# A decoder layer on one core: elementwise work moved from GpSimd to VectorE, gate products in two accumulators, LayerNorm's affine on ScalarE, conditioning dots respread

## The chip, the cores and the metric

The kernel runs on one core of a Trainium2 chip. A core has TensorE (PE in the profile, matrix products; PEld is its loading of weights), VectorE (DVE), ScalarE (ACT), GpSimd (POOL) and SyncE (SP), which here only issues transfers. Each has a queue of its own and works it off in order; they meet through semaphores. The metric is the device time of one execution in microseconds (us).

## The reference

One layer of a decoder for 1024 positions of width 1024, in float32. A mixer with a convolution and an attention branch, then a SwiGLU network; both sit between RMS norms whose shift, scale and gate come from a conditioning vector c.

```python
c_act = silu(c)
mod = c_act @ ada_w + ada_b                  # 6 x 1024 numbers
sh1, sc1, ga1, sh2, sc2, ga2 = split(mod, 6)
h = rmsnorm(x, pre_mix_g) * (1 + sc1) + sh1
proj = h @ w_in                              # conv inputs, q k v, two gates of 1024
u = u_val * sigmoid(u_gate)
u = silu(layernorm(causal_depthwise_conv(u, conv_w, conv_b)))   # width 512
y_conv = u @ w_conv_out
o = stick_breaking_attention(q, k, v)        # 8 heads of 64
y_att = o @ w_att_out
merged = sigmoid(g_conv) * y_conv + sigmoid(g_att) * y_att
x = x + ga1 * rmsnorm(merged @ w_o, post_mix_g)
h = rmsnorm(x, pre_ffn_g) * (1 + sc2) + sh2
gate, up = split(h @ w_ffn_in, 2)            # 2816 each
x = x + ga2 * rmsnorm((silu(gate) * up) @ w_ffn_out, post_ffn_g)
```

## The kernel before

**Splits.** A float32 product is made of three products of a rounded type: each operand is split into a high half (a rounding copy on ScalarE) and a low half (the difference, on another engine), and hi·hi, hi·lo and lo·hi are accumulated. Names that end in `hi` and `lo` are such halves. `load_w` (L161) loads a weight tile (128 x 1024, tile `raw`) and makes its halves; its low half is on GpSimd unless the caller names an engine. `w_op` (L297) does the same for a 128 x 512 operand that is in SBUF already, where the low half has the tile's own name (`a`, `s2o`).

**Stages.** Activations lie with channels on partitions and positions along the row; `CH` = 512 positions are half a row, `T` = 1024 a whole one. In order of time: a prologue (c, the first norm) to 60 us; the heads of the attention, with the convolution and other products as filling in TensorE's queue, to 446; the plain gates (`pg`) and the first two products of the other gates (`k1`, `k2`) to 512; the other five products of each gate pair, beside which the LayerNorm runs, to 598; `y_conv` (`pyc`) to 646; the attention's projection and the merge (`pya`) to 690; w_o (`pwo`) to 793; the first network product to 1237; and its second in three sweeps, `pa`, `pb` and `pc`, and an end, to 1476.

**Gates.** Six of the eight pairs of gate tiles are computed with seven products of half-sized operands instead of eight. `a11`, `a12`, `a21`, `a22` are the quarters of a weight tile, `s1` to `s4` sums of them, `T1` to `T4` (made from `f`) sums of quarters of h. `k1` and `k2` are done early and give `ee`; `other_five` (L586) does the rest, each product of 12 matmuls into a PSUM bank of its own out of four that rotate (`bkg`), and VectorE adds a bank to `v`, `w_` or `c21` as soon as it is done.

**LayerNorm.** `ln_all` (L626) sums channels on GpSimd (`la`), takes mean and variance by products with ones, normalizes on VectorE (`cr`), applies gain and bias on VectorE (L657), the sigmoid on ScalarE (`csig`) and the product (`csil`) on VectorE, one of four on GpSimd. `chi` and `clo` are its halves.

**Merge.** For each of eight tiles, VectorE multiplies the two halves of `pya` with the gate (`sga`), adds them to `yc` (the second half on GpSimd, L724), and the sum is split into `mhi` and `mlo` for w_o.

**Conditioning.** Each of 48 columns of `mod` is a dot of a 128 x 1024 tile of ada_w with c on VectorE (`dot_c`, L131; tiles `ada`). 0 to 15 are done in the prologue; 16 to 39 beside `y_conv` (two a step) and the merge (one a step); 40 to 47, the last gate's, in w_o.

**Order.** Loads are issued on SP's queue, stores on GpSimd's. The order of each engine's queue is set by a list scheduler of the language (`schedule_with_timeline_sim`), which simulates the program as written and takes priorities (`high_priority`); a change in one place moves rows elsewhere. Only the first network product is pinned in an order written by hand. Tiles come from pools with few buffers, and a load into a tile waits until the buffer's last reader is done: the tag `wraw` has three, `whi` and `wlo` three each. In the sweeps, `pull` issues the next steps' loads ahead, and `prep` makes the operands (`gt`, `gb`, `wa`); `w2f` are weight sums stored earlier.

Of the kernel before, what the change touches and what calls it, by code (L numbers as in the profile page):

```python
# [45 lines left out]
LN_DVE0 = ()  # L46
LN_DVE1 = ()
SILU_POOL = (3,)
# [10 lines left out]
FIN_AT = (8, 8)  # L59
W2_AT = tuple(range(EARLY, EARLY + FH))  # L60
# [13 lines left out]
def tile_block(ctx: ExitStack, tc: tile.TileContext, xT, vecs, crow, ada1, ada2, win, wv, wcv, wat, wo, w1, w2, cvw, out):  # L74
# [26 lines left out]
    def load(dst, src):  # L101
        nc.sync.dma_start(dst, src)
# [58 lines left out]
    def load_w(src, name, hi_eng=act, lo_eng=pool):  # L161
# [130 lines left out]
    HK = KT // 2  # L292
    GPAIRS = GORDER[:KT - NPL]
# [9 lines left out]
    def prod0(bank_, w, b):  # L303
        for j in range(HK):
# [7 lines left out]
            for s, (st, mv) in enumerate(((0, 0), (0, 1), (1, 0))):  # L312
                pe.matmul(bank_, w[st][:, cols], mvs[mv], start=(j == 0 and s == 0),
                          stop=(j == HK - 1 and s == 2))

    with ExitStack() as sC:
        pc = mkpool(sC, "pc")
        with ExitStack() as sA:
# [196 lines left out]
            for i in GPAIRS:  # L515
# [4 lines left out]
                prod0(k1, w_op(f"a11_{i}", raw[:, :CH], act, pool), "B11")  # L520
# [3 lines left out]
                prod0(k2, w_op(f"a12_{i}", raw[:, CH:], act, pool), "B21")  # L524
# [5 lines left out]
    with ExitStack() as sG:  # L530
# [55 lines left out]
        def other_five(i):  # L586
# [7 lines left out]
            s2o = w_op(f"s2o_{i}", s2, act, pool)  # L594
# [31 lines left out]
        def ln_all():  # L626
# [27 lines left out]
            for ct in range(CONVT):  # L654
                a = cacc[ct]
                g, b_ = vec[:, C_LNG + ct:C_LNG + ct + 1], vec[:, C_LNB + ct:C_LNB + ct + 1]
                dve.tensor_scalar(a, a, g, b_, op0=ALU.mult, op1=ALU.add)  # L657
                sg = hp.tile([P, T], F32, tag="act", name=f"csig{ct}")
                act.activation(sg, a, AF.Sigmoid, bias=0.0, scale=1.0)
# [6 lines left out]
        a2 = deque(range(2 * KT, 5 * KT))  # L666
# [9 lines left out]
        def y_conv(n):  # L676
            if n % 2 == 0:
                wcs[n // 2] = load_w(wcv[n // 2], f"wc{n}")
# [828 lines left out]
```

## Time and profile before

| | us |
|---|---|
| runs | 1476.1, 1477.73, 1478.54 (median 1477.73) |
| the profiled execution | 1477.53 |
| its span (first to last instruction) | 1475.6 |
| PE busy | 1396.4 (95%) |
| DVE busy | 1024.5 (69%) |
| ACT busy | 651.3 (44%) |
| POOL busy | 342.8 (23%) |
| mean granted clock of TensorE | 0.983 of full speed |

Busy times are sums of instructions of the profiled execution; the span is the time base of all stretches quoted below. Of POOL's time the heads' products (`be`, L459) take 100.6 us; they stay where they are.

### The profile page before, as it was taken

Reading aid. Unit: us, or ns where it says so; the run is one execution under the profiler, and the core shown is the slowest. Engines: PE = TensorE matmul, PEld = TensorE weight load, DVE = VectorE, ACT = ScalarE, POOL = GpSimd, SP = SyncE. Lnnn points to the kernel's source line nnn. Section 1 sums busy time; section 2 is a strip of 40 time slices with the busy share of each in tenths; the row PEclk is TensorE's granted clock in tenths of the full one; section 3 lists DMA queues with packets and bytes.
Section 4 is the critical chain, followed back from the end, with each engine's and each line's share of the span. In section 5 each row is a group of like instructions: output and inputs, shape, how many; then the busy total and the mean of one; then the engine's idle time right before and its main releaser. Section 6 shows DMA issues by size and latency. Waiting matters only on the chain.

```text
span 1475.6 us, 18944 instructions
## 1 busy us (share of the span) xinstructions
PE 1396.4 (95%) x6888; PEld 1164.5 (79%) x6888; DVE 1024.5 (69%) x1434; ACT 651.3 (44%) x1139; POOL 342.8 (23%) x353
## 2 busy tenths in 40 slices
PE   4999999999999899898999899999999997999996
PEld 3898788898888678686877578888888886888886
DVE  7775364545658689879668697777777765764457
ACT  5365465354554355312346543334444443433441
POOL 0042344323454564524010110001111110000000
PEclk8999999999999999999999999999999998999999
DMA  9203213122143744775823454446777759365833
GB/s 382 90 29 91 96 58 129 58 73 86 43 143 114 236 157 159 283 257 193 310 104 122 149 171 172 157 152 240 251 256 253 243 189 363 114 238 193 286 125 114
DMA packets 89356, 253.74 MB, mean 172 GB/s; under 512 B 9520, under 2 KB 19888, under 8 KB 88240
## 3 DMA queue, kind: packets, MB, share of 16 engines
q1 hardware_dynamic: 73648, 199.06, 39.8%
q0 software_dynamic: 15616, 53.49, 9.7%
q8 instruction: 54, 0.88, 0.2%
q14 instruction: 38, 0.31, 0.1%
HBM read 186.97 MB, written 65.54 MB: 171 GB/s over the span
## 4 chain that ended last, share of the span: by engine, by line
PE 30%; issue 14%; DVE 8%; POOL 3%; DMA 3%; ACT 2%; POOLq 0%; DVEq 0%; ACTq 0%
PE ka L1227 8%; PE ka L1108 6%; PE pb L1227 4%; PE kc L1108 4%; PE pwo L795 3%; PE pa L1227 2%; DMA ada<-in_ada_dram 2%; DVE ada L133 1%; POOL w_d L105 1%; PE ke L960 1%; POOL g_d L105 1%; DVE wo_lo L167 1%; DVE y L844 0%; PE psx L1004 0%; DVE yc L724 0%
## 5 line engine op out<-in xcount | busy, mean ns | idle before, releaser
L459 POOL TENSOR_TENSOR be<-be,ka 128x127 f32<-128x127 f32 (+2 forms) x96 | 100.6, 1062 | 163.0 <-DVE ka L457 90.0
L457 DVE TENSOR_TENSOR_SCAN ka<-ka 128x128 f32<-128x128 f32 (+2 forms) x96 | 106.6, 1134 | 45.5 <-ACT ka L453 45.4
L473 DVE TENSOR_TENSOR alo<-tr,ahi 128x512 fp32r<-128x512 f32 x80 | 53.1, 684 | 53.0 <-ACT ahi L472 52.3
L453 ACT ACTIVATE ka<-z 128x128 f32<-128x128 f32 (+2 forms) x96 | 47.5, 496 | 61.2 <-PE z L452 32.8
L105 POOL DMA_DIRECT2D g_d<-uw x22 | 12.0, 544 | 239.2 <-DVE uw L1180 239.2
L472 ACT ACTIVATE ahi<-tr 128x512 fp32r<-128x512 f32 x80 | 46.2, 602 | 47.0 <-PE tr L469 31.2
L1227 PE MATMUL ka<-gt,w2f 128*128 128x512 f32 x264 | 63.4, 389 | 0.0
L133 DVE SCALAR_TENSOR_TENSOR ada<-ada,cb 128x1024 f32<-128x1024 f32 x32 | 48.5, 1522 | 20.0 <-DMA ada<-in_ada_dram 19.9
L795 PE MATMUL pwo<-mhi,wo_hi 128*128 128x512 f32 x128 | 52.2, 409 | 6.7 <-ACT mhi L157 4.0
L1227 PEld LDWEIGHTS ka<-gt,w2f 128*128 128x128 f32 x264 | 49.5, 188 | 10.3
L960 PE MATMUL ke<-b,we_hi 128*128 128x512 f32 x144 | 48.0, 416 | 5.4 <-ACT we_hi L157 5.4
L795 PE MATMUL pwo<-mlo,wo_hi 128*128 128x512 f32 x128 | 51.1, 399 | 1.7 <-DVE mlo L623 1.7
L795 PE MATMUL pwo<-mhi,wo_lo 128*128 128x512 f32 x128 | 50.9, 398 | 0.5 <-DVE wo_lo L167 0.5
L469 PE MATMUL tr<-ident,be 128*128 128x128 f32 x288 | 48.8, 273 | 0.5 <-DVE alo L473 0.4
L454 ACT ACTIVATE be<-z 128x128 f32<-128x128 f32 (+2 forms) x96 | 46.9, 499 | 4.0 <-PE tr L469 3.8
L479 PE MATMUL av<-alo,vst 128*128 128x256 f32 x160 | 42.9, 294 | 2.2 <-DVE alo L473 2.1
L478 PE MATMUL av<-ahi,vst 128*128 128x256 f32 x160 | 44.8, 296 | 0.2 <-DVE oT L483 0.2
L359 PE MATMUL pcv<-ph,cvw 128*128 128x128 f32 x320 | 41.7, 276 | 1.6 <-DMA ph<-v_d 1.6
L1108 PE MATMUL kb<-b,a 128*128 128x512 f32 x156 | 41.5, 389 | 0.0
L359 PEld LDWEIGHTS pcv<-ph,cvw 128*128 128x128 f32 x320 | 39.1, 192 | 2.7 <-DMA ph<-v_d 1.7
L1227 PE MATMUL ka<-gb,wa 128*128 128x512 f32 x132 | 33.5, 402 | 7.9 <-ACT gb L157 7.9
L1213 DVE TENSOR_TENSOR gt<-X,gt 128x512 fp32r<-128x512 f32 x33 | 22.6, 691 | 26.0 <-ACT gt L157 25.9
(520 smaller groups left out, 4208.4 us busy)
## 6 DMA issues: line engine op xcount, KB each, us to landing
w_d<-w2o POOLq DMA_DIRECT2D x44, 512.0 KB, 7.1
w2f<-w_d SPq DMA_DIRECT2D x44, 512.0 KB, 4.4
ada<-in_ada_dram SPq DMA_DIRECT2D x32, 512.0 KB, 4.4
w1g<-in_w_dram SPq DMA_DIRECT2D x22, 512.0 KB, 3.6
w1u<-in_w_dram SPq DMA_DIRECT2D x22, 512.0 KB, 6.1
w2r<-in_w_dram SPq DMA_DIRECT2D x44, 256.0 KB, 3.8
cvw<-in_cvw_dram SPq DMA_DIRECT2D x20, 512.0 KB, 3.5
ada_w<-in_ada_dram SPq DMA_DIRECT2D x8, 1024.0 KB, 13.2
```

The costliest lines, as they stand in the source:

```text
L133: dve.scalar_tensor_tensor(w, w, 1.0, cb, op0=ALU.mult, op1=ALU.mult, accum_out=mod[:, col:col + 1])
L359: pe.matmul(cv[:, gi * TM:(gi + 1) * TM], wts[n][:, at:at + P], ph[:, g, SH - 1 - d:SH - 1 - d + TM], start=(d == 0), stop=(d == SH - 1))
L453: act.activation(kap[:, s_lo:s_hi], z[:, zo:zo + w], AF.Sigmoid, bias=0.0, scale=-0.125)
L454: act.activation(beta[:, :w], z[:, zo:zo + w], AF.Sigmoid, bias=0.0, scale=0.125)
L457: dve.tensor_tensor_scan(rev, rev, rev, init, op0=ALU.mult, op1=ALU.bypass)
L459: pool.tensor_tensor(beta[:, :m], beta[:, :m], kap[:, s_lo + 1:s_lo + 1 + m], op=ALU.mult)
L469: pe.transpose(tr[:, o:o + P], src, ident)
L473: dve.tensor_tensor(alo, tr, ahi, op=ALU.subtract)
L795: pe.matmul(bank_, st[:, cols], mv[k][:, cs], start=(k == 0 and q == 0), stop=(k == KT - 1 and q == 2))
L960: pe.matmul(kb, wf[st][:, cols], t[:, mv], start=(j == 0 and q == 0), stop=(j == HK - 1 and q == 2))
L1108: pe.matmul(bank_, st[:, cols], t[:, mv], start=(first and j == 0 and s == 0), stop=(j == HK - 1 and s == 2), skip_group_check=not first)
L1227: pe.matmul(dst, w[st][:, cols], g[mv], start=first and s == 0, stop=last and s == 2, skip_group_check=more)
```

## The change

Elementwise instructions that GpSimd had go to VectorE: the low halves of weights (13 in the heads' part, four each of the plain gates, the convolution's and the attention's projection), of the early gate operands (`a11`, `a12`, 12) and of the gate sums (`s1`, `s2`, `s3`, 18); the 12 sums of the LayerNorm; one silu product; two of `olo`; eight adds of the merge. GpSimd keeps the products of the heads, two low halves of `wv`, and all stores. The gate products accumulate in two banks a pair, `ka` (T2, then T3 and T4 on top) and `kc` (T1, then B22), VectorE reading a bank between. LayerNorm's gain and bias become ScalarE's: once inside the sigmoid, once as a pass of its own. Of the dots, 16 to 31 are done beside `y_conv`, none in the merge, 32 to 39 in w_o, 40 to 47 in sweep `pb` at its second to fifth step, with the conditioning vector loaded anew for each step.

```diff
-LN_DVE0 = ()
-LN_DVE1 = ()
-SILU_POOL = (3,)
+LN_DVE0 = (0, 1)
+LN_DVE1 = (0, 1)
+SILU_POOL = ()
+DOT_AT = "pb"
...
+    GP = dve
...
-    def load_w(src, name, hi_eng=act, lo_eng=pool):
+    def load_w(src, name, hi_eng=act, lo_eng=dve):
...
-    def prod0(bank_, w, b):
+    def prod0(bank_, w, b, first=True):
...
-                pe.matmul(bank_, w[st][:, cols], mvs[mv], start=(j == 0 and s == 0),
-                          stop=(j == HK - 1 and s == 2))
+                pe.matmul(bank_, w[st][:, cols], mvs[mv], start=(first and j == 0 and s == 0),
+                          stop=(j == HK - 1 and s == 2), skip_group_check=not first)
...
-                prod0(k1, w_op(f"a11_{i}", raw[:, :CH], act, pool), "B11")
+                prod0(k1, w_op(f"a11_{i}", raw[:, :CH], act, dve), "B11")
...
-            s2o = w_op(f"s2o_{i}", s2, act, pool)
+            s2o = w_op(f"s2o_{i}", s2, act, GP)
...
-            k6 = bkg(f"k6_{i}")
-            prod0(k6, s2o, "T2")
-            dve.tensor_tensor(v, k6, p1, op=ALU.add)
-            k7 = bkg(f"k7_{i}")
-            prod0(k7, w_op(f"s3o_{i}", s3, act, pool), "T3")
-            dve.tensor_tensor(w_, k7, v, op=ALU.add)
-            k4 = bkg(f"k4_{i}")
-            prod0(k4, w_op(f"a22_{i}", a22, act, dve), "T4")
-            dve.tensor_tensor(c21, k4, w_, op=ALU.add)
+            ka, kc = bkg(f"ka_{i}"), bkg(f"kc_{i}")
+            prod0(ka, s2o, "T2")
+            dve.tensor_tensor(v, ka, p1, op=ALU.add)
+            prod0(kc, w_op(f"s1o_{i}", s1, act, GP), "T1")
+            dve.tensor_tensor(w_, kc, p1, op=ALU.add)
+            prod0(ka, w_op(f"s3o_{i}", s3, act, GP), "T3", False)
+            dve.tensor_tensor(w_, ka, w_, op=ALU.add)
+            sig_out(w_, 2 * i + 1, 1)
+            prod0(kc, w_op(f"s4o_{i}", s4, act, dve), "B22", False)
+            dve.tensor_tensor(v, kc, v, op=ALU.add)
+            sig_out(v, 2 * i, 1)
+            prod0(ka, w_op(f"a22_{i}", a22, act, dve), "T4", False)
+            dve.tensor_tensor(c21, ka, p1, op=ALU.add)
             sig_out(c21, 2 * i + 1, 0)
-            k5 = bkg(f"k5_{i}")
-            prod0(k5, w_op(f"s1o_{i}", s1, act, pool), "T1")
-            dve.tensor_tensor(v, k5, v, op=ALU.add)
-            dve.tensor_tensor(w_, k5, w_, op=ALU.add)
-            k3 = bkg(f"k3_{i}")
-            prod0(k3, w_op(f"s4o_{i}", s4, act, dve), "B22")
-            dve.tensor_tensor(v, k3, v, op=ALU.add)
-            sig_out(v, 2 * i, 1)
-            sig_out(w_, 2 * i + 1, 1)
...
-                dve.tensor_scalar(a, a, g, b_, op0=ALU.mult, op1=ALU.add)
-                act.activation(sg, a, AF.Sigmoid, bias=0.0, scale=1.0)
+                act.activation(sg, a, AF.Sigmoid, bias=b_, scale=g)
+                act.activation(a, a, AF.Identity, bias=b_, scale=g)
...
-        a2 = deque(range(2 * KT, 5 * KT))
+        a2 = deque(range(2 * KT, 4 * KT))
...
-                (pool if c and n < Y_POOL else dve).tensor_tensor(y[:, cs], y[:, cs], sg[c], op=ALU.add)
+                dve.tensor_tensor(y[:, cs], y[:, cs], sg[c], op=ALU.add)
...
-            ada2_dots(last, 1)
...
-                for col in ((), (40, 41), (42, 43), (44, 45), (46,), (47,), ())[n]:
+                for col in ((), (32, 33), (34, 35), (36, 37), (38,), (39,), ())[n]:
...
+        def gate_dots(n):
+            cbt = wp.tile([P, D], F32, tag="wraw", name=f"cb_{n}")
+            load(cbt, cb_d)
+            for q in range(2):
+                w = wp.tile([P, D], F32, tag="wraw", name=f"ada2_{40 + n + q}")
+                load(w, ada2[24 + n + q])
+                dot_c(w, cbt, 40 + n + q)
...
+                if name == DOT_AT and 0 < j <= KT // 2:
+                    gate_dots(2 * j - 2)
```

The built programs show where the rows went. First VectorE's queue at the early gate products, where `ee_i` is the sum of pair i's first two products, `f` and `T` the sums of h, `a_i` the low half of an early gate operand; before:

```order
L565 TENSOR_TENSOR f_3_4727<-f_3_4728,f_3_4727 128x512
L525 TENSOR_TENSOR ee_1_4454<-k_1_4473,ee_1_4453 128x512
L566 TENSOR_TENSOR f_3_4728<-f_3_4728,f_3_4727 128x512
L567 TENSOR_TENSOR f_3_4728<-f_3_4728 128x512
L556 TENSOR_TENSOR T2o_4735<-f_3_4728,T2o_4735 128x512
L556 TENSOR_TENSOR T3o_4738<-f_3_4727,T3o_4738 128x512
L592 TENSOR_TENSOR gs_0_4759<-gw0b 128x512
```

And the same place of the changed kernel:

```order
L567 TENSOR_TENSOR f_3_4727<-f_3_4728,f_3_4727 128x512
L568 TENSOR_TENSOR f_3_4728<-f_3_4728,f_3_4727 128x512
L302 TENSOR_TENSOR a_4_4579<-ew_4574,a_4_4579 128x512
L569 TENSOR_TENSOR f_3_4728<-f_3_4728 128x512
L558 TENSOR_TENSOR T2o_4735<-f_3_4728,T2o_4735 128x512
L558 TENSOR_TENSOR T3o_4738<-f_3_4727,T3o_4738 128x512
L558 TENSOR_TENSOR T1o_4741<-f_3_4727,T1o_4741 128x512
L302 TENSOR_TENSOR a_4_4597<-ew_4574,a_4_4597 128x512
L527 TENSOR_TENSOR ee_1_4454<-k_1_4473,ee_1_4453 128x512
L558 TENSOR_TENSOR T4o_4744<-f_3_4728,T4o_4744 128x512
```

The low halves `a` stand between the sums, and the add of pair 1 has moved behind the sums of h that it stood before. (On TensorE, 126 matmuls of the plain gates stand behind the last product of the attention instead of 93.) Second, VectorE's queue in the merge; before:

```order
L723 TENSOR_TENSOR sga_1_5885<-pya_1_5887,sga_1_5885 128x512
L133 SCALAR_TENSOR_TENSOR ada_33_5922,mod<-ada_33_5922,cb 128x1024
L724 TENSOR_TENSOR yc_5543<-yc_5543,sga_0_5884 128x512
L723 TENSOR_TENSOR sga_0_5931<-pya_0_5933,sga_0_5931 128x512
L723 TENSOR_TENSOR sga_1_5932<-pya_1_5934,sga_1_5932 128x512
L133 SCALAR_TENSOR_TENSOR ada_34_5969,mod<-ada_34_5969,cb 128x1024
L623 TENSOR_TENSOR mlo_5919<-yc_5543,mhi_5918 128x1024
L724 TENSOR_TENSOR yc_5585<-yc_5585,sga_0_5931 128x512
```

After:

```order
L720 TENSOR_TENSOR sga_0_5939<-pya_0_5941,sga_0_5939 128x512
L720 TENSOR_TENSOR sga_1_5940<-pya_1_5942,sga_1_5940 128x512
L620 TENSOR_TENSOR mlo_5936<-yc_5561,mhi_5935 128x1024
L721 TENSOR_TENSOR yc_5597<-yc_5597,sga_0_5939 128x512
L721 TENSOR_TENSOR yc_5597<-yc_5597,sga_1_5940 128x512
L168 TENSOR_TENSOR wo_0_lo<-wo_0_raw,wo_0_hi 128x1024
```

Both adds of a step stand in VectorE's queue now, and the dots are gone from between them. Third, VectorE's queue where sweep `pa` ends and `pb` begins (`wa_10` are the low halves of `pa`'s last weight tile, `gt` those of `pb`'s operands), after:

```order
L134 SCALAR_TENSOR_TENSOR ada_40_10881,mod<-ada_40_10881,cb_10879 128x1024
L1208 TENSOR_TENSOR gt_0_10835<-X_10330,gt_0_10835 128x512
L1265 TENSOR_TENSOR X_10330<-Y_10341,X_10330 128x512
L1265 TENSOR_TENSOR X_10330<-X_10330 128x512
L1214 TENSOR_TENSOR wa_10_10742<-wa_10679,wa_10_10742 128x512
L1208 TENSOR_TENSOR gt_0_10839<-X_10330,gt_0_10839 128x512
L134 SCALAR_TENSOR_TENSOR ada_41_10884,mod<-ada_41_10884,cb_10879 128x1024
L1214 TENSOR_TENSOR wa_10_10748<-wa_10679,wa_10_10748 128x512
```

And on SP's queue there, where the loads of the dots stand between those of `w2f`:

```order
L103 DMA cb_10879<-cb_d 128x1024
L103 DMA w2f_0_10718<-w_d_122 128x1024
L103 DMA w2f_0_10720<-w_d_122 128x1024
L103 DMA ada_40_10881<-in_ada_dram 128x1024
L103 DMA w2f_1_10736<-w_d_123 128x1024
L103 DMA w2f_1_10738<-w_d_123 128x1024
L103 DMA ada_41_10884<-in_ada_dram 128x1024
L103 DMA cb_10924<-cb_d 128x1024
```

The second low half of `wa_10` stands behind two dots, the second of which waits for a load that can only start when the first dot has freed its buffer; before, no dot stood in this stretch.

More of the change, by code (lines that the diff above doesn't have):

```diff
@@ L523, in tile_block @@
                 k2 = bank(f"k2_{i}")
-                prod0(k2, w_op(f"a12_{i}", raw[:, CH:], act, pool), "B21")
+                prod0(k2, w_op(f"a12_{i}", raw[:, CH:], act, dve), "B21")
                 dve.tensor_tensor(e[1], k2, e[0], op=ALU.add)
@@ L677, in y_conv @@
             if n % 2 == 0:
-                wcs[n // 2] = load_w(wcv[n // 2], f"wc{n}")
+                wcs[n // 2] = load_w(wcv[n // 2], f"wc{n}", act, dve)
             y = flat(ot(f"yc{n}"))
@@ L863, in tile_block @@
                         dot_c(w, cb2, col)
-        add_bias(40, 48)
-        fold_gate(gpost2, 40, C_POST2)
+        add_bias(32, 40)
+        fold_scale(scale2, 32, C_PRE2)
         begin = len(nc.cur_bb.bb.instructions)
@@ L1388, in tile_block @@
             act.activation(c22[n], kc[n], AF.Copy)
+        add_bias(40, 48)
+        fold_gate(gpost2, 40, C_POST2)
         sweep("pc", prep3, (False, False), kc)
```

7 lines of the change are left out of this document (3 added, 4 removed).

## The prediction

> **What bounds the kernel now.** I read the engines' shares first, then the busy time by stage, then TensorE's waits, and last the rows of the engines waited for.
>
> ```profile
> PE 1396.4 (95%) x6888; PEld 1164.5 (79%) x6888; DVE 1024.5 (69%) x1434; ACT 651.3 (44%) x1139; POOL 342.8 (23%) x353
> 60.00:455.00 395.00, 388.39 (x2415) 339.76 (x2414) 222.51 (x274) 206.91 (x423) 152.88 (x124) 1.00 0.25 81
> 455.00:500.00 45.00, 40.07 (x169) 32.36 (x168) 40.89 (x40) 20.00 (x38) 23.45 (x23) 0.96 0.47 154
> 500.00:590.00 90.00, 89.65 (x388) 72.48 (x387) 73.77 (x90) 43.09 (x68) 49.39 (x47) 1.00 0.52 177
> 590.00:608.00 18.00, 11.67 (x38) 7.21 (x37) 17.05 (x15) 8.79 (x11) 10.03 (x8) 0.91 0.68 265
> 608.00:690.00 82.00, 81.59 (x360) 67.19 (x358) 67.75 (x83) 17.06 (x17) 32.50 (x14) 1.00 0.76 260
> 690.00:712.00 22.00, 15.70 (x52) 11.55 (x53) 18.57 (x23) 6.92 (x8) 6.56 (x3) 0.77 0.34 109
> 980.00:1237.00 257.00, 257.00 (x1136) 212.87 (x1135) 190.68 (x303) 114.55 (x205) 38.47 (x72) 1.00 0.69 240
> 1307.00:1370.00 63.00, 63.00 (x280) 52.16 (x279) 35.33 (x53) 22.97 (x39) 0.00 (x0) 1.00 0.72 246
> ```
>
> The first row is the page's; the others give a stretch, its length, the busy time (and instructions) of PE, PEld, DVE, ACT and POOL, the granted clock, the DMA share and GB/s. TensorE is the bound: it is full in most stages, and a change of the other engines can only win back its holes. Full pace is 257.00 / 1136 = 0.226 us for a matmul. By that count the early k products (455 to 500) lose 45 − 169 × 0.226 = 6.8 us, the passage from the gate products to the convolution's projection (590 to 608) 18 − 38 × 0.226 = 9.4, and the passage from the attention's projection to w_o (690 to 712) 22 − 52 × 0.226 = 10.2. In those three VectorE is busy for 91%, 95% and 84% of the time. The 395 us of heads lose only 395 − 388.39 = 6.6. So 26.4 us lie where this change works.
>
> ```profile
> PE k L313 <- DVE ee L525: 4.9, 2, 2.6
> PE pwo L795 <- ACT mhi L157: 4.0, 2, 3.8
> PE pyc L178 <- ACT chi L157: 2.9, 2, 2.7
> PE k L313 <- DVE s4o L300: 2.1, 1, 2.1
> PE pwo L795 <- DVE mlo L623: 1.7, 2, 1.2
> 495.70:499.10 3.40, 3.40 (x10) 2.71 (x9) 1.41 (x1) 1.25 (x3) 3.17 (x4) 0.51 1.01 342
> 598.10:601.50 3.40, 3.21 (x7) 2.05 (x8) 2.74 (x3) 3.20 (x4) 2.55 (x2) 0.51 0.49 191
> 697.00:707.30 10.30, 6.09 (x14) 4.43 (x15) 9.72 (x12) 3.06 (x3) 4.18 (x2) 0.51 0.03 12
> ```
>
> The waits (us, times, longest) name what TensorE stood for: results of VectorE, or a rounding on ScalarE that itself stood for VectorE. The three stretches of half clock say what the waits cost on top: 3.4 us at 0.51 loses 1.7 us, 10.3 us loses up to 5.
>
> The Trainium skill, "TensorE: Matmul & The Clock Gate", section "What's actually happening", lets the clock halve after at least one idle window of about 3.4 us. Here longest waits of 2.6 and 2.7 us already stand near a half-clock stretch, so the trace halves earlier than that page says. By its rule a residual wait under 3.4 us would cost itself alone, and the sum below would be 1.7 us lower.
>
> **The k products.** The two waits on `ee` (4.9 us) are adds that come late in VectorE's queue because their neighbours are stretched.
>
> ```profile
> 469.96 1.71 POOL L300 TENSOR_TENSOR a<-ew,a 128x512 fp32r<-128x512 f32 x1
> 470.43 1.78 DVE L564 TENSOR_TENSOR f<-f 128x512 f32<-128x512 f32 x1
> 474.09 0.69 DVE L566 TENSOR_TENSOR f<-f,f 128x512 f32<-128x512 f32 x1
> L525 DVE TENSOR_TENSOR ee<-k,ee 128x512 f32<-128x512 f32 x6 | 4.1, 686 | 2.9 <-DMA s_d<-ee 2.9
> L300 POOL TENSOR_TENSOR a<-ew,a 128x512 fp32r<-128x512 f32 x10 | 15.1, 1515 | 16.9 <-ACT a L157 9.0 <-issue 7.8
> L643 DVE TENSOR_TENSOR cr<-cr,lm 128x512 f32<-128x512 f32 x8 | 8.5, 1125 | 0.0
> L562 DVE TENSOR_TENSOR f<-hhi,hlo 128x1024 f32<-128x1024 f32 x3 | 5.8, 1949 | 0.0
> L657 DVE TENSOR_SCALAR cr<-cr,vec 128x1024 f32<-128x1024 f32 x4 | 4.1, 1050 | 0.0
> L662 DVE TENSOR_TENSOR csil<-cr,csig x3: 2144/2195/3630, 585.5 to 593.2; 128x1024 f32<-128x1024 f32 x3
> ```
>
> The first three rows are the timeline, the rest groups of 455 to 608 (behind the bar: us busy, mean ns) and, last, a tile's row (min, median and max ns). Beside a GpSimd elementwise an add of VectorE takes 1.78 us; alone 0.69. The add that reads PSUM (`ee`, 686 ns) is not touched. So a 128x512 op taken from GpSimd frees up to 1.1 us of VectorE and costs 0.69 there.
>
> For 455 to 608 as a whole, VectorE's busy time before is 40.89 + 73.77 + 17.05 = 131.7 us. Added: ten `a` lows, 18 gate-operand lows and 12 LayerNorm adds, 40 × 0.69 = 27.6; three convolution-weight lows at 1.22 (the `mlo` row below, 128x1024) 3.7; one silu product, 2.2 (the median of its three siblings). Removed: L657, 4.1; six gate adds, 4.1. The stretching goes: summed over the 21 groups of this view that exceed 0.69 or 1.22 us without reading PSUM (L643 is the first, at 8 × 0.44; L562 gives 3 × 0.73) it is about 30 us. That leaves 131.7 + 33.5 − 8.2 − 30 = 127 us. TensorE's own work there is (169 + 388 + 38) × 0.226 = 134.5 us, and about 33 matmuls of plain gates, which the new order leaves until after the last attention product, add 7.5 us of cover at its start. VectorE thus has less to do than TensorE, not more. I take the full 6.8 us back; the bounds are 0 (the `a` lows now stand ahead of `ee` in one queue) and 6.8.
>
> **LayerNorm and the two-bank gate products.** ScalarE gains four 128x1024 passes, about 1.06 us each (`mhi` below is such a pass), and has 18 − 8.79 = 9.2 us free in 590 to 608, so they fit; yet they stand in the chain sigmoid, product, rounding, low half, four times, in which VectorE has 4 × (2.2 + 1.22) = 13.7 us and ScalarE 4 × 3 × 1.06 = 12.7. Two banks instead of five make the third product of a pair wait until VectorE has read the first's bank; between them stands the other bank's product of 12 × 0.226 = 2.7 us, or another pair's, against a read of 0.69. That is covered while VectorE lags under 2 us. The end of the chain has no such cover to spare, so I leave one wait of 1.7 us and one 3.4 us stretch at half clock, 1.7 us: 3.4 of 9.4 remain, 6.0 come back. Bounds: all 9.4 back; or 5 lost, if each of the last pairs waits about one read.
>
> **Attention's projection.** The merge loop is where VectorE is the bound.
>
> ```profile
> 658.65 1.28 DVE L723 TENSOR_TENSOR sga<-pya,sga 128x512 f32<-128x512 f32 x2
> 701.86 0.68 DVE L723 TENSOR_TENSOR sga<-pya,sga 128x512 f32<-128x512 f32 x1
> L723 DVE TENSOR_TENSOR sga<-pya,sga 128x512 f32<-128x512 f32 x16 | 10.6, 680 | 0.0
> L724 POOL TENSOR_TENSOR yc<-yc,sga 128x512 f32<-128x512 f32 x8 | 17.1, 2138 | 31.8 <-DVE sga L723 31.8
> L133 DVE SCALAR_TENSOR_TENSOR ada<-ada,cb x32: 1207/1226/4272, 609.7 to 740.9; 128x1024 f32<-128x1024 f32 x32
> L157 ACT ACTIVATE mhi<-yc x8: 1057/1061/1065, 661.7 to 705.5; 128x1024 fp32r<-128x1024 f32 x8
> L623 DVE TENSOR_TENSOR mlo<-yc,mhi x8: 1209/1226/2299, 663.8 to 706.6; 128x1024 fp32r<-128x1024 f32 x8
> L178 PE MATMUL pya<-ohi,wa_hi x64: 389/389/389, 645.9 to 688.3; 128*128 128x512 f32 x64
> ```
>
> From the first `sga` to the last, VectorE takes (701.86 − 658.65) / 7 = 6.2 us a step, TensorE 24 × 0.226 = 5.4. It begins late too: the first products (from 645.9) end about 651.3, the first `sga` starts at 658.65, a lag of 7.3. After the change a step is 2 × 0.68 + 2 × 0.69 + 1.23 = 4.0 us, and with two weight lows, three `wo` lows and some left-over dots (about eight of 1.2 us in eight steps) near 5: it now keeps pace, catching up 0.4 to 1.4 us a step. After seven steps the lag is 0 to 4.5. The last step's own chain is 0.68 + 0.69 + 1.06 + 1.23 = 3.7 us, under w_o matmuls on the earlier tiles. The eight dots that go to the convolution's part stand there twice a step as before, and eight that were in w_o give place to eight others. I take 8.0 of the 10.2 back; bounds 4 and 10.2.
>
> **The dots in sweep pb.** Eight dots, eight loads of 512 KB for them and four reloads of the conditioning vector enter a stage that loses nothing now.
>
> ```profile
> 1303.10 0.69 DVE L1219 TENSOR_TENSOR wa<-wa,wa 128x512 fp32r<-128x512 f32 x1 [1.49 <-ACT wa L157]
> ada<-in_ada_dram SPq DMA_DIRECT2D x32, 512.0 KB, 4.4
> ada_w<-in_ada_dram SPq DMA_DIRECT2D x8, 1024.0 KB, 13.2
> ```
>
> Busy time is no matter: 8 × 1.31 = 10.5 us against 63 − 35.33 = 27.7 free. The bytes raise 246 GB/s by 6.3 MB / 63 us = 100 GB/s, under the 342 GB/s that stood at a DMA share of 1.01 in the row of 495.7 above, but near it. What can hurt is order. The tiles rotate through three buffers, so the second dot's load waits for the first dot, and the next vector's load for the second. VectorE issues in order, and behind the second dot stands the last low half of `wa` (1303.10 before, so finished 1303.8), which TensorE needs at the sweep's start, about 1307 where the last stretch of the first fence begins. One round is 4.4 us of landing and 1.3 of dot. SP issues in order too: the waiting loads stand ahead of `w2f` of the third to sixth step, each step being 24 × 0.226 = 5.4 us of products, so a round costs a step of the lead that `w2f` has. The sweep's loads start early enough that I expect one short stop in its first half: 2.5 us lost, between 0 and 7 (one load landing 4.4 us late, plus half clock after it).
>
> **The heads.** Thirteen weight lows go to VectorE, where the scans of the attention stand.
>
> ```profile
> L459 POOL TENSOR_TENSOR be<-be,ka 128x512 f32<-128x512 f32 x32 | 42.3, 1336 | 58.7 <-ACT be L454 35.2 <-DVE ka L457 17.4 <-PE z L452 3.7
> L167 POOL TENSOR_TENSOR wgv_lo<-wgv_raw,wgv_hi 128x1024 fp32r<-128x1024 f32 x4 | 9.6, 2402 | 39.9 <-ACT wgv_hi L157 39.9
> ```
>
> VectorE has 395 − 222.5 = 172 us free and takes 13 × 1.22 = 16, at most 13 × 2.56 = 33 if each meets a `be` product (1.34). GpSimd's queue, which holds the `be` products on the attention's chain, loses blocks of 2.4 us each. A scan can now be late by a low half instead. I set it at 0, between a loss of 6 (half the lows delay an attention step by 1 us) and a gain of 4 out of 6.6.
>
> The Trainium skill, "SBUF — State Buffer", section "SBUF: two separate sides", calls the pair of ports that VectorE and GpSimd share an exclusive lock held for a whole instruction, the loser fully blocked. The 1.78 against 0.69 agrees in kind. By it the lows moved to VectorE in the heads are blocked, not slowed, and block the `be` products in turn: a loss of some 6 us rather than 0, as at the bad end just given.
>
> **The sum.** −6.8 − 6.0 − 8.0 + 2.5 + 0 = −18.3 us. The profiled execution took 1477.53 us (span 1475.6), within 0.2 of the median 1477.73, so the forecast is 1459.2 us.
>
> **Rivals.** First, all is recovered: the three holes and 4 us of the heads with nothing lost in pb give 1477.5 − 26.4 − 4 = 1447; half-way to it 1451. The 127 against 134.5 us speaks for it; 9.4 us of holes at a chain's end, seldom fully closed, against. Chance 0.13.
>
> Second, VectorE becomes the bound of the gate stage: GpSimd was a second worker, and each low now queues behind an unrelated add. If the ee adds and the LayerNorm chain come as late as before (their 12.8 us not had), only w_o gains: 1477.5 − 8.0 + 2.5 = 1472; with half of them, 1466. For it speaks that the margin is 7.5 us in 134; against, that 30 us of stretching must go. Chance 0.20, about 1469.
>
> Third, the other side: the dots in pb. If a load there lands in 13.2 us, as the 1 MB ones did, instead of 4.4, three rounds in which VectorE stands cost 3 × 8.8 = 26 us, and the change ends at 1459.2 + 26 − 2.5 = 1483: slower. It decides when a landing exceeds about 10 us, since three times (10 − 4.4) is 17, about the gain. DMA share 0.72 speaks for longer landings, the 4.4 median at a share of 0.76 (608 to 690) against. Chance 0.08.
>
> Fourth, the new order starves the heads: the 33 moved matmuls are fillers which the attention's own waits then lack, 7.5 us of idleness there: 1467. The scheduler orders by its own times, so I give it 0.07.
>
> **How the numbers follow.** The forecast, 1453 to 1465, has 0.52. The range takes it, the second and the fourth rival and most of the first: 1447 to 1473. Two executions of this kernel differ by about 0.2% (3 us), so within 1474.8 to 1480.7 counts as the same. Faster is the forecast, first and fourth rival, and nearly all of the second: 0.87; the same 0.05; slower the third rival, 0.08.
>
> **What would show it.** In the changed profile: no wait on `ee` and full clock at 470 to 515; VectorE's 128x512 adds at 0.69 from the heads' end on; about 3 us lost before `pyc`; `sga` steps of 5.4 us, paced by TensorE, and under 3 us lost before `pwo`; one stop in pb behind a dot that waited for a load. Wrong would be: a VectorE above 95% busy through the gates with TensorE waiting for `w_op` lows (second rival), landings of 10 us in pb (third), TensorE holes before 446 us (fourth).

## The result, and the profile after

The changed kernel takes 1457.84 us (median; 1456.9 to 1458.78), the one before 1478.13 on the same chip: a ratio of 0.986, interval 0.9839 to 0.9881. Forecast were 1459.2 and a range of 1447 to 1473. The profiled execution took 1457.92 us with a span of 1456.1, 19.5 less than before.

The page's first row and the stretches of the page before (same columns; from 500 on everything comes earlier than before, so a stretch with the same bounds holds other work; the row of 670 to 690 was not among before's):

```profile
PE 1389.9 (95%) x6888; PEld 1162.5 (80%) x6888; DVE 1021.7 (70%) x1503; ACT 658.6 (45%) x1143; POOL 193.2 (13%) x275
60.00:455.00 395.00, 387.61 (x2416) 339.71 (x2415) 237.65 (x298) 207.51 (x424) 107.20 (x105) 1.00 0.25 81
455.00:500.00 45.00, 44.32 (x195) 36.08 (x194) 35.71 (x54) 22.20 (x40) 6.54 (x13) 1.00 0.49 169
500.00:590.00 90.00, 86.36 (x369) 68.53 (x368) 77.22 (x113) 54.10 (x76) 10.16 (x19) 1.00 0.58 208
590.00:608.00 18.00, 18.00 (x82) 14.88 (x81) 10.66 (x15) 5.92 (x7) 1.62 (x3) 1.00 0.46 150
670.00:690.00 20.00, 18.21 (x79) 14.11 (x78) 14.52 (x19) 7.07 (x7) 0.00 (x0) 1.00 0.33 106
690.00:712.00 22.00, 22.00 (x99) 18.22 (x98) 12.13 (x16) 9.80 (x15) 0.00 (x0) 1.00 1.03 391
1307.00:1370.00 63.00, 63.00 (x280) 52.18 (x279) 31.61 (x49) 25.50 (x43) 0.00 (x0) 1.00 0.86 317
```

GpSimd lost 150 us of busy time, and VectorE, which took its work over, has 1021.7 against 1024.5: less, not more. The clock is full in all stretches shown. The early products are nearly full (45 − 195 × 0.226 = 0.9 us lost, where it was 6.8). The convolution's projection `pyc` now starts at 583.5 and w_o at 679.1, so the rows of 590 to 608 and 690 to 712 lie behind the two passages; the passage to w_o is in the row of 670 to 690, where TensorE is idle for 1.8 us. A new loss stands in 500 to 590, where it is idle for 90 − 86.36 = 3.6 us. Its waits between 455 and 720 (us, times, longest):

```profile
PE ka L315 <- ACT s2o L158: 2.3, 2, 1.7
PE pwo L790 <- ACT mhi L158: 1.5, 1, 1.5
PE ka L315 <- DVE gw L606: 1.2, 1, 1.2
PE ka L315 <- DVE gv L602: 0.8, 2, 0.6
PE pwo L790 <- DVE sga L720: 0.3, 1, 0.3
```

The waits on `ee`, `chi`, `clo` and `mlo` are gone. Where the time went is read best from the ends of TensorE's stages. The tile rows of the changed kernel (ns min, median, max; then the first and last start):

```profile
L179 PE MATMUL pg<-hhi,wg_lo x64: 387/389/475, 419.8 to 467.4; 128*128 128x512 f32 x64
L179 PE MATMUL pyc<-chi,wc_lo x64: 389/389/389, 584.9 to 635.0; 128*128 128x512 f32 x64
L790 PE MATMUL pwo<-mhi,wo_lo x128: 388/389/502, 679.7 to 774.6; 128*128 128x512 f32 x128
```

Before, these last starts were 466.9, 645.7 and 793.5. So from the last `pg` to the last `pyc` ("gates" below) it takes 167.6 us instead of 178.8, from there to the last `pwo` ("merge and w_o") 139.6 instead of 147.8, and the rest to the end of the span 681.5 instead of 682.1. The heads end 0.5 later. −11.2 − 8.2 − 0.6 + 0.5 = −19.5, the difference of the spans. The same three lengths, from the same rows, sort out the experiments:

| kernel | gates | merge and w_o | rest | median us | ratio to before (interval) |
|---|---|---|---|---|---|
| before | 178.8 | 147.8 | 682.1 | 1478.13 | |
| changed | 167.6 | 139.6 | 681.5 | 1457.84 | 0.986 (0.9839 to 0.9881) |
| changed, again | 170.6 | 138.7 | 683.7 | 1459.90 | 0.9856 (0.9841 to 0.987) |
| e1 merge adds on GpSimd | 168.6 | 139.9 | 684.0 | 1460.56 | 0.986 (0.9844 to 0.9877) |
| e2 dots as before | 167.5 | 146.2 | 681.6 | 1463.92 | 0.9885 (0.9864 to 0.9906) |
| e3 both | 167.6 | 146.4 | 683.5 | 1466.11 | 0.9896 (0.9881 to 0.9911) |
| e5 gate lows on GpSimd | 178.2 | 139.7 | 683.4 | 1467.70 | 0.991 (0.9895 to 0.9924) |
| e8 idle work on GpSimd | 183.9 | 139.8 | 684.5 | 1473.70 | 0.9937 (0.992 to 0.9953) |
| e6 LayerNorm as before | 174.2 | 138.7 | 683.9 | 1464.96 | 0.988 (0.9865 to 0.9895) |
| e4 five banks | 165.6 | 137.0 | 682.9 | 1454.42 | 0.981 (0.9796 to 0.9825) |
| e7 heads' lows on GpSimd | 167.2 | 137.0 | 683.7 | 1457.47 | 0.9829 (0.9814 to 0.9844) |
| e11 heads' and gate lows on GpSimd | 176.6 | 140.9 | 682.1 | 1467.09 | 0.99 (0.9884 to 0.9917) |
| e10 dots in pa | 168.8 | 138.4 | 690.7 | 1468.66 | 0.9908 (0.9894 to 0.9923) |
| e9 e4 and e7 together | 163.7 | 137.0 | 681.6 | 1450.40 | 0.9792 (0.9777 to 0.9807) |

The lengths are of one profiled execution each. Where the program is the same (the rest, in all but before, e2, e3 and e10), they differ by up to 3 us, and the gates of the two executions of the changed kernel differ by 3.0. The profiled executions of e5, e6, e8 and of the changed kernel's second run were the slowest of their four, 1.9 to 3.6 us over the median, so their lengths are rather too long. Chips differ too (the kernel before has medians of 1478.1 to 1482.8), so times of different chips are compared by the ratios.

### The profile page after: what moved, and what is told of

The parts are those of the page before. It is cut to its first block, busy times and chain, and to the rows that moved or that the text cites. A ratio compares the mean times of both kernels' runs of the same rounds, so it can differ in the third digit from the quotient of the medians.

```text
span 1456.1 us, 18905 instructions
## 1 busy us (share of the span) xinstructions
PE 1389.9 (95%) x6888; PEld 1162.5 (80%) x6888; DVE 1021.7 (70%) x1503; ACT 658.6 (45%) x1143; POOL 193.2 (13%) x275
## 4 chain that ended last, share of the span: by engine, by line
issue 46%; PE 43%; POOL 6%; DMA 2%; DVE 2%; ACT 1%; POOLq 0%; SPq 0%; DVEq 0%; ACTq 0%
PE ka L1222 8%; PE pb L1222 4%; PE pg L179 3%; PE pgv L179 3%; PE pv L381 3%; PE pcv L361 3%; PE pgg L179 2%; PE pq L179 2%; PE pk L179 2%; PE pa L1222 2%; PE tr L471 2%; POOL w_d L106 2%; POOL g_d L106 2%; PE av L481 1%; PE av L480 1%
## 5 line engine op out<-in xcount | busy, mean ns | idle before, releaser
L459 DVE TENSOR_TENSOR_SCAN ka<-ka 128x128 f32<-128x128 f32 (+2 forms) x96 | 95.2, 1015 | 40.1 <-ACT ka L455 40.0
L134 DVE SCALAR_TENSOR_TENSOR ada<-ada,cb 128x1024 f32<-128x1024 f32 x32 | 39.0, 1222 | 17.5 <-DMA ada<-in_ada_dram 17.3
L1103 PE MATMUL ka<-b,a 128*128 128x512 f32 x156 | 39.7, 389 | 0.0
```

The source lines that it names most:

```text
L459: dve.tensor_tensor_scan(rev, rev, rev, init, op0=ALU.mult, op1=ALU.bypass)
L1103: pe.matmul(bank_, st[:, cols], t[:, mv], start=(first and j == 0 and s == 0), stop=(j == HK - 1 and s == 2), skip_group_check=not first)
```

## The experiments

**The merge: adds or dots** (e1, e2, e3). The prediction gave VectorE's shorter step 8 us, without saying which of the two edits in it counts.

```diff
 # e1
-                dve.tensor_tensor(y[:, cs], y[:, cs], sg[c], op=ALU.add)
+                (pool if c else dve).tensor_tensor(y[:, cs], y[:, cs], sg[c], op=ALU.add)
 # e2 (e3 has both)
-        a2 = deque(range(2 * KT, 4 * KT))
+        a2 = deque(range(2 * KT, 5 * KT))
...
+            ada2_dots(last, 1)
...
-DOT_AT = "pb"
+DOT_AT = ""
```

> The changed kernel with one edit undone: the second add of each merge step is GpSimd's again (8 adds); the dots stay out of the merge. Theory (VectorE was the bound of the merge by its work per step): a step is 2 x 0.68 + 0.69 + 1.23 = 3.3 us plus stretched neighbours, some 4.4 with left-overs, under TensorE's 5.4, so the pace holds, and only the last step's chain is longer, by 2.1 - 0.69 = 1.4 us: 1457.8 + 1.5 = 1459.3 (0 to +3). Rival (the gain of the merge was GpSimd's slow adds): all 8.2 us of the merge are lost, 1466.

> The changed kernel with the dots as before: one a step in the merge again, columns 40 to 47 in w_o, none in sweep pb; the merge adds stay VectorE's. Theory: a step of VectorE is 4.0 + 1.31 + left-overs, near 5.9 against 5.4 of TensorE, from a late start: 3 to 5 us lost before w_o, nothing won in pb (it lost nothing): 1457.8 + 4 = 1462 (1460 to 1464). Rival (the adds alone made the gain): 1457.8. Rival (the dots in pb cost something): 1456 or less.

> Both of the two edits before together: merge adds on GpSimd and dots as before. Theory: the merge is the one of the kernel before, 6.2 us a step, so its 8.2 us are lost: 1466 (1464 to 1468), more than the two edits apart add up to. Rival (the lag came from the gates before it, which are still mended): 1460.

With the adds back on GpSimd the merge and w_o grow by 0.3 us, which is nothing; with the dots back in the merge by 6.6; with both by 6.8. In the merge the dots made the gain, the adds none of it. The rows are e1's add, e2's wait, and the first and last `sga` of the changed kernel:

```profile
L721 POOL TENSOR_TENSOR yc<-yc,sga x8: 1614/1670/2202, 646.6 to 685.2; 128x512 f32<-128x512 f32 x8
```

```profile
PE pwo L792 <- DVE sga L720: 5.6, 1, 5.6
```

```profile
L720 DVE TENSOR_TENSOR sga<-pya,sga x16: 677/681/686, 646.4 to 683.1; 128x512 f32<-128x512 f32 x16
```

A GpSimd add takes 1.67 us. The rounding of `mhi` on ScalarE waits for it, but TensorE hardly does: its waits on `sga` and `mhi` before w_o are 2.4 us in e1 and 1.8 in the changed kernel. In e2, w_o's first product stands 5.6 us for the last `sga`, because with a dot a step VectorE is behind. In the changed kernel the steps take (683.1 − 646.4) / 7 = 5.2 us: TensorE's 5.4 less the catching up of a late start. By the times e2 loses less than by this stage, 0.25% or 3.7 us, and the intervals of e2 and the changed kernel overlap; that is about the 4 us expected. e3 came out at the 1466 expected, but its stage loses 6.8 us, no more than its parts (0.3 and 6.6).

**The gates: stretching, or slow results** (e5, e8). In e5, the 30 low halves of the gate products are GpSimd's again; in e8 VectorE keeps them, and GpSimd gets 30 instructions whose output is not used.

```diff
 # e5
-    GP = dve
+    GP = pool
-                prod0(k1, w_op(f"a11_{i}", raw[:, :CH], act, dve), "B11")
+                prod0(k1, w_op(f"a11_{i}", raw[:, :CH], act, pool), "B11")
...
 # e8, in w_op
+        if name[:3] in ("a11", "a12", "s1o", "s2o", "s3o"):
+            pool.tensor_tensor(junk, t[:, 0], t[:, 0], op=ALU.add)
```

> The changed kernel with the 30 low halves of the gate products (12 of the early operands, 18 of the sums) on GpSimd again. Theory (GpSimd's elementwise stretches VectorE's): each takes 0.69 us off VectorE and adds 1.1 us by stretching a neighbour, 12 us more VectorE work in a stage with 7.5 us of margin: the hole at the early products comes back: 1457.8 + 7 = 1465 (1462 to 1468). Rival (a second worker is welcome once the rest is moved): 1455 to 1458.

> The changed kernel with 30 idle instructions added on GpSimd, at the places where the kernel before had the low halves of the gate products: each adds the high half of an operand to itself and writes a tile that nobody reads. VectorE keeps its work. Theory (stretching): VectorE's 128x512 instructions beside them go from 0.69 to about 1.8 us, 30 x 1.1 = 33 us more on VectorE in a stage with 7.5 us of margin, so 10 to 25 us are lost: 1468 to 1483. Rival (the gain came from shorter chains, results no longer made by a slow engine): 1458, no change.

The first rows of the two pages, e5's and then e8's:

```profile
PE 1396.3 (95%) x6888; PEld 1164.1 (79%) x6888; DVE 1021.3 (70%) x1473; ACT 657.1 (45%) x1143; POOL 238.6 (16%) x305
```

```profile
PE 1395.9 (95%) x6888; PEld 1163.2 (79%) x6888; DVE 1041.8 (71%) x1503; ACT 657.3 (45%) x1143; POOL 232.3 (16%) x305
```

e8 shows the stretching by itself: the same 1503 instructions of VectorE take 1041.8 instead of 1021.7 us, 20.1 more, 0.67 for each idle instruction (1.1 was expected), and the gates of its profiled execution take 16.3 us more, longer than in the kernel before (by the ratios the whole kernel loses 0.8%, some 11 us). How a stretched instruction reaches TensorE stands in e8's rows: two groups of VectorE by mean duration (behind the bar: us, mean ns), then a piece of the timeline.

```profile
L304 DVE TENSOR_TENSOR s2o<-gs,s2o 128x512 fp32r<-128x512 f32 x6 | 7.0, 1162 | 0.2 <-ACT s2o L158 0.2
L531 DVE TENSOR_TENSOR ee<-k,ee 128x512 f32<-128x512 f32 x6 | 4.1, 682 | 4.1 <-DMA s_d<-ee 4.1
```

```profile
486.16 1.53 DVE L562 TENSOR_TENSOR T3o<-f,T3o 128x512 fp32r<-128x512 f32 x1
487.61 1.52 DVE L562 TENSOR_TENSOR T1o<-f,T1o 128x512 fp32r<-128x512 f32 x1
490.39 0.50 PE L319 MATMUL k<-hhi,a 128*128 128x512 f32 x1 [3.10 <-DVE ee L531]
```

The low half `s2o` takes 1162 ns on average (693 in the changed kernel), the add `ee`, which reads PSUM, is not stretched. Two sums of h take 1.5 us each beside GpSimd, `ee` stands behind them, and TensorE waits 3.1 us for it. No operand comes from GpSimd there, so the rival that only the shorter chains counted is out. (The idle instructions also stand ahead of GpSimd's stores. VectorE's one wait for a store of `ee`, 4.1 us, ends at 513.8, in a stretch in which TensorE is full; what else the stores add is not told apart.) e5 is the other side of it: VectorE has 30 instructions of 0.69 us fewer, 20.7 us, and yet is busy 1021.3 us. What GpSimd took off it came back as stretching, to within 0.4 us. Still e5 loses 10.6 us in the gates of its profiled execution, nearly all that the change had won there, and 0.5% or 7 us by the ratios; the time is within the range expected, but the wait on `ee` is only 0.5 us, so it is not the hole at the early products that was expected. Since VectorE's sum is unchanged, that loss must lie in when results come: its waits in the gates name low halves and late adds.

```profile
PE ka L315 <- ACT s2o L158: 2.7, 2, 2.3
PE ka L315 <- DVE gv L602: 2.1, 1, 2.1
PE lnv L647 <- DVE la L645: 2.0, 1, 2.0
PE ka L315 <- POOL s2o L302: 1.3, 1, 1.3
PE ka L315 <- DVE gw L606: 1.0, 2, 0.8
PE k L315 <- DVE ee L527: 0.5, 2, 0.3
```

How much of it is stretching at a bad moment and how much GpSimd's own 1.3 to 1.7 us for a low half, no run separates.

**The LayerNorm** (e6).

```diff
-LN_DVE0 = (0, 1)
-LN_DVE1 = (0, 1)
-SILU_POOL = ()
+LN_DVE0 = ()
+LN_DVE1 = ()
+SILU_POOL = (3,)
...
+                dve.tensor_scalar(a, a, g, b_, op0=ALU.mult, op1=ALU.add)
-                act.activation(sg, a, AF.Sigmoid, bias=b_, scale=g)
-                act.activation(a, a, AF.Identity, bias=b_, scale=g)
+                act.activation(sg, a, AF.Sigmoid, bias=0.0, scale=1.0)
```

> The changed kernel with the LayerNorm as before: its 12 sums and one silu product on GpSimd, gain and bias on VectorE (4 x 0.81 us). Theory: VectorE loses 12 x 0.69 + 2.2 and gains 3.2 and up to 12 x 1.1 of stretching; the convolution's projection, which in the changed trace starts without a wait, is the first thing to come late: +2 (0 to +5), 1460. Rival (the LayerNorm moves brought most of the gates' gain): 1465 or more. Rival (they cost ScalarE's chain something): 1455.

The gates of the profiled execution lose 6.6 us; by the ratios the whole kernel loses 0.2%, some 3 us, with overlapping intervals, so the size is not clear of noise, and whether 0 to 5 was right stays open. The place was not the one expected: no wait before `pyc`, but eleven waits inside the gate products and the LayerNorm, these the most of them:

```profile
PE ka L315 <- DVE gw L606: 3.1, 3, 1.7
PE ka L315 <- DVE gv L602: 2.4, 2, 1.3
PE kc L315 <- DVE s1o L302: 1.2, 2, 1.0
```

VectorE gave away 12 × 0.69 + 2.2 and took 4 × 0.80, 7.3 us less of its own, and was busy 5.6 us longer:

```profile
PE 1395.7 (95%) x6888; PEld 1163.7 (79%) x6888; DVE 1027.3 (70%) x1494; ACT 653.1 (45%) x1139; POOL 215.5 (15%) x288
```

So 13 instructions of GpSimd stretched VectorE's by about 13 us.

**The two banks** (e4). The diff is the one of `other_five` above, read backwards, with `GP` for `pool`.

> The changed kernel with the gate products in separate banks again (five a pair, six adds instead of five), all else as changed. Theory (the relief of VectorE brought the gain of the gates, and the two banks cost waits): the stops of TensorE at the pairs' starts, 4.8 us over the pace in the changed trace, shrink by half, six more adds of 0.69 cost nothing: 1455.5 (1453 to 1458). Rival (the two banks brought it): 3 to 10 us lost, 1461 to 1468.

The gates get 2.0 us shorter; the waits on `gv` and `gw` are gone, and those left between 455 and 650 are

```profile
PE pyc L179 <- DVE clo L625: 1.8, 1, 1.8
PE k L315 <- ACT s2o L158: 0.9, 1, 0.9
PE pyc L179 <- DVE gc L608: 0.5, 1, 0.5
```

The two banks did not bring the gain; they cost some of it, since the third product of a pair waits for the read of the first. How much is less sure: 2.0 us in the gates, and another 2.6 in merge and w_o, where TensorE has no wait left before w_o (1.8 us in the changed kernel); by the ratios it is 0.5% or 7 us, clear of both intervals of the changed kernel. The time of 1454.42 us is within the range expected.

**The heads and the early products** (e7, e11). e7 changes the default of `load_w` back (17 low halves), e11 adds e5's edits.

```diff
-    def load_w(src, name, hi_eng=act, lo_eng=dve):
+    def load_w(src, name, hi_eng=act, lo_eng=pool):
```

> The changed kernel with the low halves of the heads' weights and of the plain gates (13 and 4) on GpSimd again. The heads lost 0.5 us by the change in the traces. Theory: the heads are full either way: 1457.8 (1456.5 to 1459.5). Rival (the lows in VectorE's queue delay the attention's scans, the lock): 1453 to 1456, faster.

> The changed kernel with all weight lows of the heads, the plain gates and the gate products on GpSimd again (17 and 30). With the gate lows alone on GpSimd (10.6 us lost, all after 506 us) and with the heads' lows alone (nothing lost) the early products k1, k2 ran without a hole of `ee`. Theory (two things mended that hole, the relief of VectorE and the 33 plain-gate matmuls that stand behind the attention; either is enough): with both gone the hole of about 6 us before 500 us comes back, beside the loss of the later gates: 1457.8 + 10.6 + 6 = 1474 (1470 to 1478). Rival (the hole was mended by VectorE's other order): 1468.

The heads don't care: 0.4 us between e7 and the changed kernel at the last `pg`, and the changed kernel's own two executions differ by 0.5 there. By the ratios e7 is 0.3% or 4 us ahead, at the edge of the intervals; what its trace wins is behind the heads (2.6 us in merge and w_o), so the rival's lock on the scans is not the reason. e7's order leaves fewer plain-gate products behind the attention. The last product of the attention, before, in the changed kernel, in e7 and in e11:

```profile
L479 PE MATMUL av<-alo,vst x160: 274/283/387, 91.0 to 445.9; 128*128 128x256 f32 x160
```

```profile
L481 PE MATMUL av<-alo,vst x160: 274/282/388, 92.5 to 438.9; 128*128 128x256 f32 x160
```

```profile
L481 PE MATMUL av<-alo,vst x160: 274/282/388, 91.4 to 446.8; 128*128 128x256 f32 x160
```

```profile
L481 PE MATMUL av<-alo,vst x160: 274/282/389, 92.5 to 447.3; 128*128 128x256 f32 x160
```

With these, four kernels make a square for the hole at the early products: neither cover nor relief of VectorE (e11), cover alone (e5), relief alone (e7), both (changed). Of these only e11 has the wait of the kernel before:

```profile
PE k L315 <- DVE ee L527: 3.3, 2, 2.6
```

In e5 it is 0.5 us, in the other two it is not there. So in these four either was enough. A fifth kernel bounds that: e8 has the cover (its last product of the attention starts at 438.6), but its VectorE keeps the low halves and is stretched as well, and the wait on `ee` is back with 3.7 us. VectorE is busy for 41.0 of the 45 us from 455 to 500 there and 41.45 in e11, 40.89 in the kernel before; in e5, e7 and the changed kernel it is 32.03 to 38.37. In these runs cover helped only where VectorE was not that full.

e11 as a whole is not slower than e5: 176.6 us of gates against 178.2, where 1474 us was expected and 1467 came, the rival's number but not its reason, for the hole is there. The waits say that TensorE stopped early instead of late: those on `gv`, `gw`, `s2o` and the LayerNorm's sums are 6.6 us in e11 and 9.1 in e5. A likely reading, not tested by itself, is that an early stop of TensorE lets VectorE catch up; the two losses did not add up.

**The dots in another sweep** (e10).

```diff
-DOT_AT = "pb"
+DOT_AT = "pa"
```

> The changed kernel with its eight dots of columns 40 to 47 in sweep pa instead of pb (steps 2 to 5), where the weight tiles wa pass through the same three buffers and their low halves stand behind the dots on VectorE. Theory (a dot that waits in order for its load delays what stands behind it by landing time less cover; in pb the cover was there, in pa each step needs a wa and two lows of 0.69 on VectorE): a round of 4.4 to 7 us of landing a step against a step of 5.4 us of products: 1 to 2 us a step, four steps, and half clock: 1464 (1460 to 1472). Rival (loads are early enough everywhere): 1458.

About 9 us are lost (1468.66 against 1459.90 us on the same chip), in the rest. First the chain in `pb` of the changed kernel, on VectorE:

```profile
1283.54 1.23 DVE L134 SCALAR_TENSOR_TENSOR ada<-ada,cb 128x1024 f32<-128x1024 f32 x1 [1.19 <-DMA ada<-in_ada_dram]
1284.69 0.08 DVE L134 DVE_READ_ACCUMULATOR ada<-ada,cb 128x1 f32 x1
1284.69 0.69 DVE L1214 TENSOR_TENSOR wa<-wa,wa 128x512 fp32r<-128x512 f32 x1
```

The second dot waits 1.19 us for its load, the low half of `wa` stands behind it, as forecast, and TensorE, still in `pa` until 1288.1, does not notice. In e10 TensorE's waits in `pa`, then the rows that the second wait goes back to, and those of the first:

```profile
PE ka L1222 <- ACT wa L158: 3.0, 1, 3.0
PE ka L1222 <- DVE gb L1208: 2.2, 1, 2.2
```

```profile
1235.52 1.22 DVE L134 SCALAR_TENSOR_TENSOR ada<-ada,cb 128x1024 f32<-128x1024 f32 x1 [6.77 <-DMA ada<-in_ada_dram]
1237.28 1.89 DVE L1208 TENSOR_TENSOR gb<-X,gb 128x512 fp32r<-128x512 f32 x3
1238.01 3.61 PE L1222 MATMUL ka<-gb,wa 128*128 128x512 f32 x8 [2.25 <-DVE gb L1208]
```

```profile
1269.16 1.23 DVE L134 SCALAR_TENSOR_TENSOR ada<-ada,cb 128x1024 f32<-128x1024 f32 x1 [0.76 <-DMA ada<-in_ada_dram]
```

```profile
1270.43 3.16 SPq L103 DMA_DIRECT2D wa<-in_w_dram  x3
```

```profile
1274.08 1.15 ACT L158 ACTIVATE wa<-wa 128x512 fp32r<-128x512 f32 x2 [6.25 <-DMA wa<-in_w_dram]
```

VectorE stands 6.77 us in front of a dot whose load is not there, the low halves `gb` stand behind it, and TensorE waits 2.2 us for one of them: this is the order that the expectation named. The other stop, 3.0 us, comes by the three shared buffers: the weight tile's load is issued when a dot has freed a buffer (1269.16 + 1.23), and its rounding on ScalarE stood 6.25 us for it. Both made the loss, with half clock behind each stop (a granted clock of 0.77 from 1238 to 1245 and 0.76 from 1275 to 1282). The size was as expected (0.5% in the ratios, some 8 us, against 6).

**The version that is faster than both** (e9): e4 and e7 together, beside the changed kernel again on the same chip.

> The changed kernel with five banks a pair again and the low halves of the heads' weights and of the plain gates on GpSimd again, each of which alone was no slower than the changed kernel. Theory (the two banks only cost; GpSimd's lows in the heads meet little VectorE work): 1454 (1452 to 1456), faster than the changed kernel by 0.2 to 0.4%. Rival (with GpSimd's lows the early products lose their cover of plain gates and the five banks do not help that): 1458.

> The changed kernel as it is, beside the three others of this call on one chip: 1457 to 1460.

1450.4 against 1459.9 us, 2.1% under the kernel before (ratio 0.9792, 0.9777 to 0.9807) where the changed kernel has 0.9856 (0.9841 to 0.987). That is more than was expected (1452 to 1456), and the intervals are apart. The gates take 163.7 us, and of waits in them and before w_o nothing over 0.6 us is left.

## Why the prediction was right, point by point

- **The bound** (TensorE, with 26.4 us of holes in reach) held: 19.5 us came back, all but 0.1 of it in the stretches named.
- **VectorE's sum over 455 to 608** was forecast as 127 us instead of 131.7. Measured are 35.71 + 77.22 + 10.66 = 123.6, but the same bounds now end 24.5 us behind the start of `pyc` (583.5) instead of 10 (598.0), so the two sums are not of the same work. The stretching did go: the subtraction of the mean, 1125 ns before, is now

```profile
L640 DVE TENSOR_TENSOR cr<-cr,lm 128x512 f32<-128x512 f32 x8 | 5.0, 681 | 0.0
```

- **Early products**, 6.8 us back: right in size, 5.9 by the forecast's own count. The step named two causes, relief and 7.5 us of cover; by the square of e5, e7, e11 and the changed kernel either alone would have done, and by e8 the cover alone fails when VectorE gets fuller.
- **Gates and passage to `pyc`**, 6.0 back: measured 11.2 − 6.8 = 4.4. The forecast residue of 3.4 us is 5.0, but not where the step put it. It judged the two banks covered and left the loss at the end of the LayerNorm's chain. `pyc` starts without a wait, and the residue is the stops on `s2o`, `gw` and `gv`. The step "that is covered while VectorE lags under 2 us" was where it failed: TensorE waited 2.0 us for the reads (`gw` 1.2, `gv` 0.8), and without the two banks (e4) the kernel is faster by 2.0 us in the gates and by 0.5% as a whole. That the end came out near the forecast all the same is in part luck: the loss left for the LayerNorm's chain did not come, and one of about the same size came from the banks and `s2o`.
- **Merge and w_o**, 8.0 back: measured 8.2. What the sum did not say is that the dots are 6.6 of it and the adds 0.3; the remaining 1.4 (both undone in e3 lose 6.8) no run places.
- **Sweep pb**, 2.5 lost: measured nothing; from the last `pa` to the last product on `gt` in `pb` it is 59.9 us after and 59.8 before. The mechanism stood there as described; the term was too large because `pa`'s remaining products cover it. Landings were longer than the 4.4 us used; the transfers of 1270 to 1350 have

```profile
ada<-in_ada_dram SPq DMA_DIRECT2D x8, 512.0 KB, 7.2
```

  as their median. The last pair took 10.0 us, the size from which the third rival was to decide, and still without a loss: the rival counted three rounds in which VectorE stands, but the loads of a step after the first were issued together and the sweep's weights had been loaded ahead. e10 shows the loss that threatened, in another place, in part by the order and in part by the buffers.
- **Heads**, 0: measured +0.5, and undoing it in e7 cost another 0.4; neither is more than two executions of the changed kernel differ. VectorE's busy time there grew by 237.65 − 222.51 = 15.1 us, under the lower of the two estimates (16 and 33). The lows hardly met `be` products, and with GpSimd's lows gone the attention's own scans got shorter: the 48 of 128x512 take 1296 ns on average instead of 1481, which the step had not counted. The harm of 6 us that the Trainium skill's rule of an exclusive lock ("SBUF — State Buffer", section "SBUF: two separate sides") would have brought did not come.
- **The half clock.** The forecast added 1.7 us for a stretch of half clock behind one short wait. In the first profile of the changed kernel there was none in the gates; in the second there was one, which cost 3 us (below).

## What to carry to other kernels

Before handing an elementwise instruction to a second engine, add up what it does to the first: here 30 subtractions on GpSimd saved VectorE 20.7 us of instructions and cost it the same in stretching, so the help was none, and TensorE waited for the results besides. That is a matter of the place: of the 20.7 us that the 17 low halves of e7 take off VectorE, 10.5 remained (1011.2 against 1021.7 us), and the fastest version has them on GpSimd. Where several edits share a gain, undo them one at a time, for the one that looks like the cause (the slow adds of the merge) may be worth 0.3 us and its neighbour (the dots) 6.6; and a mended place can carry an edit that only costs (two banks). An instruction that waits in order for a transfer is harmless where TensorE still has products in front of it, and costs where TensorE soon needs what stands behind it, or where the tiles it holds are the ones the next step is loaded into.

## What the runs showed of the hardware

The same wait does not always bring half clock. Two executions of the same changed kernel, the stretch of 521 to 532 us in each, both with a wait of TensorE on `s2o` of 1.7 us and one on `gv` of 0.6:

```profile
521.00:532.00 11.00, 8.77 (x38) 6.50 (x37) 10.67 (x18) 5.68 (x10) 1.62 (x3) 1.00 0.42 144
```

```profile
521.00:532.00 11.00, 8.74 (x25) 6.18 (x24) 9.62 (x17) 4.53 (x9) 1.08 (x2) 0.69 0.39 117
```

Busy for the same time, TensorE did 38 matmuls in the one and 25 in the other, at a granted clock of 1.00 and 0.69: 13 × 0.226 = 2.9 us, most of the 3.0 us by which the gates of the second execution are longer. The Trainium skill, "TensorE: Matmul & The Clock Gate", section "What's actually happening", has the clock follow a free-running window of observation; that would let the same wait fall differently in two executions, but no run here shows the window itself. The idle window of about 3.4 us that it names for the half clock does not agree with these traces, the waits here being 1.7 and 0.6 us with four matmuls between them. A short wait is therefore priced with a chance of half clock, not with a fixed sum.

GpSimd's stretching has also a price that depends on the neighbours: 0.67 us of VectorE for each idle instruction in e8, about 1.0 for each of the LayerNorm's in e6, where the first row of contention shown in the prediction was 1.1. The adds that read PSUM were not stretched in any of these traces (`ee`: 686 ns before, 682 in e8).
